# A hybrid decoder layer: two attention rates set to 0.93 and 0.95, and five wide raw-weight buffers in place of four

## The chip, the cores and the metric

The kernel runs on one core of one Trainium2 chip. The metric is the device time of one execution in microseconds (us), the median of three runs. Before the change it is 2094.58 us (2094.41 to 2095.52).

## The reference

One layer over 1024 tokens of width 2048, all in float32:

```python
h = rmsnorm(x, g_pre);  u = h @ w_in          # one projection, its columns cut into parts
log_a = log_sigmoid(g_lr @ w_a2 + b_a) / 16
o_gla = rmsnorm(gla_chunked(gq, gk, gv, log_a), g_head) * silu(g_gate)   # 4 heads, dk 128, dv 256
z = sq @ sk.T * 128**-0.5                                                # 8 heads, dh 128
w = sigmoid(z) * exp(suffix sum of log_sigmoid(-z)), for s < t           # stick-breaking
o_sb = (w @ sv) * silu(s_gate)
x = x + rmsnorm(concat(o_gla, o_sb) @ w_out, g_post)
x = x + sigmoid(x @ w_g + b_g) * (p @ w_p)
```

## The kernel before, in words

Every dense product of float32 is made of three TensorE products. A matrix is split into a rounded part and a rest (`split`: an ACT copy and a DVE subtraction, lines 112 and 113), and rounded x rounded, rest x rounded and rounded x rest are summed in PSUM. Acts are `ah` and `al`; narrow weights are `raw`, split into `hi` and `lo`; wide weights (128x1024, from `wload2`, line 874) are `wr`, split into `wh` and `wl`.

The work has three stretches.

1. **Projections with attention between them.** `dense` runs 38 units of 96 matmuls each, and calls `step()` sixteen times in a unit, once after every six matmuls (the last time behind the evacuation). `step()` adds `rate[1]` to an account and advances the attention's generator once for each whole in it. So `rate[1]` is the number of attention steps for one dense step, and it alone places the attention's instructions among the matmuls. First the four GLA heads come, at rate 1.0, then `sb()`, the stick-breaking attention of eight heads, at 1.0 until the second head's projections are there and at `RATE_SB` from then on. A head can't begin before its three units are done (`while h not in sb_ready`): it spends steps on waiting. A head takes 38 attention steps: 2, and 6 for each of six items. An item is two score blocks one step apart, then, 8 steps after, `turned` (the transposed weights copied and split into `s`, of which there are two pairs of buffers), and 8 further on `values` (the product with v), once or twice (two steps apart).
2. **The end of the attention.** After the last unit, `rate[1]` is `RATE_TAIL`. Twelve small products of the gate's weights (24 matmuls and four steps each) run with what is left of the attention, 48 steps in all. Beside them `x_set` loads eight tiles (`u<-S2x_d`) and splits them (`ah<-u`), then eight of `S1x_d`. What is then left of the attention is written out at once, with no matmul of the products between (line 816: `while urgent or jobs or beside`; called the drain below). Four more small products follow.
3. **Wide products**, one level of a Strassen-like scheme for the gate, `w_out` and `w_g`. `product` takes 24 matmuls; weights are prepared ahead: `wload2` loads, `sub` and `add` (lines 869 and 872) combine blocks, `wsplit` splits. In some loops a round of two products loads three blocks and stores one or two combinations. There are four `wr` buffers. In the last loops `embed` makes six more matmuls from a narrow weight (`pr`, split into `ph` and `pl`).

Nearly all DMAs are issued from SP, in one queue in the order of the program that the scheduler makes (a transpose of attention, `E<-X`, too); ACT, DVE and PE also run in that order. PE's order is that of the steps above.

Of the kernel before, what the change touches and what calls it, by code (L numbers as in the profile page):

```python
# [44 lines left out]

RATE_GLA = 1.0
W0, W1, W2 = 3, 6, 1
RATE_SB = 0.9
W3 = 4
V_MID, V_END, VW = ("X", "X"), ("E", "E"), 3  # L50
L1, L2, PERIOD = 8, 8, 5
# [1 line left out]
KP = KT // 2  # L53
LAG = 10
RATE_BG = 0.5
RATE_TAIL = 1.1
LAST_11 = 4
PACE_QKV, PACE_TAIL = 15, 4

# [2 lines left out]
def layer(ctx, tc, xT, w_in, w_gate, w_lr, w_a2, b_a, g_pre, g_head, w_out, g_post,  # L62
# [24 lines left out]
    def nm(base):  # L87
        serial[0] += 1
        return f"{base}_{serial[0]}"
# [76 lines left out]
    def advance(queue):  # L166
        while queue:
            if next(queue[0], None) is not None:
                return True
            queue.popleft()  # L170
        return False
# [42 lines left out]
    with tc.tile_pool(name="start", bufs=1) as sp:  # L214
# [24 lines left out]
        for q in range(4):  # L239
            w = [wload(w_in[n, q]) for n in range(2)]  # L240
            for kk in range(4):
                k = 4 * q + kk
                sl = slice(kk * P, (kk + 1) * P)
                for hf in HALVES:
                    raw = sp.tile([P, HT], F32, tag="xraw", name=nm("xraw"), bufs=20)
# [30 lines left out]
    with tc.tile_pool(name="att", bufs=1, reuse_waits="tile") as ap:  # L276
# [441 lines left out]
        for u, (h, i) in enumerate(flat):  # L718
# [18 lines left out]
            if i == len(heads[h]) - 1:  # L737
                if h < GLA_HEADS:
                    jobs.append(gla(h, heads[h][0], heads[h][1], heads[h][2:]))
                else:  # L740
                    sb_ready[h - GLA_HEADS] = heads[h]
                    if h == GLA_HEADS:
                        jobs.append(sb())
                    rate[1] = RATE_SB if h > GLA_HEADS else rate[1]

# [10 lines left out]
        def x_set(name, hf):  # L756
            for k in range(8):
                t = at("u")
                dma2(t, part(sx_d[name][k // 2], k))
                yield 1  # L760
                if k % 2 == 0:
                    wides = act_wide(hf, k // 2)
                pair = tuple(part(x, k) for x in wides)
                split(*pair, t)
                g_sets[name].append(pair)
# [38 lines left out]
        while beside:  # L804
            advance(beside)
        rate[1], pace[1] = RATE_TAIL, PACE_TAIL
        beside.append(x_set("S2", 1))
# [17 lines left out]
    def mt(tag, bufs, n=W, dt=F32, name=None):  # L825
        pool = keep if tag == "ar" else mp if tag in ("wr", "wh", "wl", "cw") else late[0]
        return pool.tile([P, n], dt, tag=tag, name=nm(name or tag), bufs=bufs)
# [12 lines left out]
    if True:  # L840
# [31 lines left out]
            V.tensor_tensor(dst, a, b, op=ALU.subtract)  # L872

        def wload2(src):
            raw = mt("wr", 4)
            dma(raw, src)
            return raw

# [142 lines left out]
        for j in range(8):  # L1021
            with ahead():
                b11, t1, t2 = (wload2(w_gate[kh, nh, j]) for kh, nh in ((0, 0), (0, 1), (1, 1)))
                sub(t1, t1, b11)
                sub(t2, t1, t2)
                w2, w1 = wsplit(t2), wsplit(t1)
                add(b11, b11, t2)
                dma2(t2_d[j], t2)
                dma2(t3_d[j], b11)
            p = product(g_sets["S2"], w2)  # L1030
            with soon():
                add(u(j), p, part(u1_s[j // 2], j) if j < 6 else u(j))
            p = product(g_sets["S1"], w1)
            with soon():
                add(v(j), p, u(j))
# [5 lines left out]
        for j in range(8):  # L1041
            with ahead():
                t4, t2 = wload2(w_gate[1, 0, j]), wload2(t2_d[j])
                add(t4, t4, t2)
                w = wsplit(t4)
            p = product(x_act[1][8:], w)
            with soon():
                add(u(j), p, u(j))
        drain()

        for j in range(8):
            with ahead():
                w = wsplit(wload2(t3_d[j]))
            p = product(sets["S3"], w)
            gate(j, 1, p, u(j))
            gate(8 + j, 1, p, v(j))
# [308 lines left out]
```

## Time and profile before

| | us |
|---|---|
| median of three runs | 2094.58 |
| the profiled execution | 2091.95 |
| its span, first to last instruction | 2089.9 |
| PE busy | 2068.4 |
| DVE busy | 1487.0 |
| ACT busy | 875.6 |

Matmuls overlap in the trace, so PE's busy time isn't its work. What tells whether PE loses time is how far apart matmuls start and how many of them fall into a stretch: a stretch of wide products alone holds 222 in 50 us. The projections end and the end of the attention begins at about 1097 us; the wide products begin at 1203 us.

### The profile page before, as it was taken

The numbers are of one execution on the slowest core, as the hardware profiler recorded it, in microseconds if no ns is written. First come the engines' busy times: TensorE is split into PE (matmuls) and PEld (weight loads), VectorE is DVE, ScalarE is ACT, GpSimd is POOL, SyncE is SP. The second block draws the span as 40 slices with busy tenths as digits, with TensorE's granted clock in tenths as the row PEclk, the third lists the DMA queues.
The fourth block names the chain that finished last, engine by engine and source line by source line (L and its number), as shares of the span: only waits on it lengthen the run. The fifth ranks groups of instructions, "written<-read, shape, count | busy, mean of one in ns | idle before, by whom it ended". The sixth has DMA issues, their size and how long they took to land.

```text
span 2089.9 us, 26754 instructions
## 1 busy us (share of the span) xinstructions
PE 2068.4 (99%) x9712; PEld 1708.3 (82%) x9712; DVE 1487.0 (71%) x2243; ACT 875.6 (42%) x1390; POOL 106.5 (5%) x228
## 2 busy tenths in 40 slices
PE   9999999999999999999999999999999999999998
PEld 6788888888888888888888788888888888787887
DVE  8657777676767667666567667788777787876665
ACT  7433333343455455555456413344233434323332
POOL 3100000000011011101001000000000000000000
PEclk9999999999999999999999999999999999999999
DMA  6222222222244344433336687888877586876663
GB/s 217 69 69 74 85 74 85 67 85 67 72 113 105 93 99 121 107 100 97 78 84 152 211 307 282 317 316 289 329 288 261 182 322 216 304 266 213 226 199 113
DMA packets 229812, 352.81 MB, mean 169 GB/s; under 512 B 124464, under 2 KB 129456, under 8 KB 229680
## 3 DMA queue, kind: packets, MB, share of 16 engines
q1 hardware_dynamic: 229104, 349.01, 52.1%
q10 hardware_dynamic: 576, 2.10, 0.3%
q8 instruction: 76, 1.25, 0.3%
q14 instruction: 56, 0.46, 0.1%
HBM read 249.85 MB, written 73.92 MB: 155 GB/s over the span
## 4 chain that ended last, share of the span: by engine, by line
PE 50%; DVE 9%; DMA 8%; issue 2%; ACT 2%; POOL 0%; SPq 0%; DVEq 0%; ACTq 0%; POOLq 0%
PE dn L101 45%; DMA wr<-w_g 3%; PE z L101 2%; PE t L101 2%; DVE wl L113 2%; DMA E<-X 2%; DMA wr<-w_out 1%; PE o L101 1%; DVE wr L872 1%; DVE al L113 1%; DMA ar<-og_d 1%; DVE ar L869 1%; DVE X L599 1%; DVE wr L869 1%; DVE ev L869 0%
## 5 line engine op out<-in xcount | busy, mean ns | idle before, releaser
L101 PE MATMUL dn<-ah,hi 128*128 128x512 f32 x1408 | 563.2, 400 | 1.5 <-ACT hi L112 1.3
L101 PE MATMUL dn<-al,hi 128*128 128x512 f32 x1408 | 551.0, 391 | 0.2 <-DVE al L253 0.2
L101 PE MATMUL dn<-ah,lo 128*128 128x512 f32 x1408 | 550.8, 391 | 0.2 <-DVE lo L113 0.2
L101 PE MATMUL dn<-ah,wl 128*128 128x512 f32 x1216 | 474.1, 390 | 2.2 <-DVE wl L113 2.2
L101 PE MATMUL dn<-al,wh 128*128 128x512 f32 x1216 | 473.7, 390 | 0.0
L101 PE MATMUL dn<-ah,wh 128*128 128x512 f32 x1216 | 473.7, 390 | 0.0
L101 PEld LDWEIGHTS dn<-ah,hi 128*128 128x128 f32 x1408 | 265.8, 189 | 60.7 <-ACT ah L252 3.4
L101 PEld LDWEIGHTS dn<-al,hi 128*128 128x128 f32 x1408 | 264.9, 188 | 58.1 <-DVE al L253 0.9
L101 PEld LDWEIGHTS dn<-ah,lo 128*128 128x128 f32 x1408 | 265.9, 189 | 48.2 <-DVE lo L113 0.5
L112 ACT ACTIVATE wh<-wr 128x1024 fp32r<-128x1024 f32 x152 | 158.9, 1056 | 307.5 <-DVE wr L872 150.1
L101 PEld LDWEIGHTS dn<-ah,wl 128*128 128x128 f32 x1216 | 228.4, 188 | 51.2 <-DVE wl L113 4.0
L101 PEld LDWEIGHTS dn<-ah,wh 128*128 128x128 f32 x1216 | 228.4, 188 | 47.6
L101 PEld LDWEIGHTS dn<-al,wh 128*128 128x128 f32 x1216 | 228.4, 188 | 47.0
L113 DVE TENSOR_TENSOR wl<-wr,wh 128x1024 fp32r<-128x1024 f32 x152 | 185.1, 1219 | 6.5 <-ACT wh L112 6.4
L112 ACT ACTIVATE hi<-raw 128x512 fp32r<-128x512 f32 x192 | 119.8, 626 | 147.3 <-PE dn L101 141.2
L113 DVE TENSOR_TENSOR lo<-raw,hi 128x512 fp32r<-128x512 f32 x192 | 134.7, 703 | 57.7 <-ACT hi L112 57.3
L329 ACT ACTIVATE X<-E 128x256 uint16<-128x256 uint16 (+2 forms) x96 | 81.0, 843 | 126.5 <-DVE E L604 118.9
L599 DVE TENSOR_TENSOR_SCAN X<-X 128x128 f32<-128x128 f32 (+2 forms) x96 | 98.3, 1024 | 30.9 <-POOL X L593 21.0
L872 DVE TENSOR_TENSOR wr<-wr,wr 128x1024 f32<-128x1024 f32 x48 | 58.7, 1224 | 76.4 <-issue 25.0
L614 DVE COPY v<-E 128x512 uint16<-128x512 uint16 (+1 forms) x160 | 63.6, 429 | 55.6 <-DMA E<-X 45.8
L869 DVE TENSOR_TENSOR wr<-wr,wr 128x1024 f32<-128x1024 f32 x48 | 58.8, 1224 | 46.9 <-DMA wr<-w_g 31.8
L113 DVE TENSOR_TENSOR s<-v,s 128x512 fp32r<-128x512 f32 (+1 forms) x82 | 52.3, 638 | 43.2 <-ACT s L112 39.6
(245 smaller groups left out, 2293.0 us busy)
## 6 DMA issues: line engine op xcount, KB each, us to landing
raw<-w_in SPq DMA_DIRECT2D x160, 256.0 KB, 2.7
wr<-w_g SPq DMA_DIRECT2D x64, 512.0 KB, 4.3
wr<-w_out SPq DMA_DIRECT2D x56, 512.0 KB, 4.8
wr<-w_gate SPq DMA_DIRECT2D x40, 512.0 KB, 5.2
g_d<-wr SPq DMA_DIRECT2D x32, 512.0 KB, 2.7
wr<-g_d SPq DMA_DIRECT2D x32, 512.0 KB, 4.9
ar<-h_d SPq DMA_DIRECT2D x28, 512.0 KB, 5.0
ar<-og_d SPq DMA_DIRECT2D x25, 512.0 KB, 4.8
```

The source lines that it names most:

```text
L101: PE.matmul(o, lhsT, rhs, start=start, stop=stop)
L112: A.activation(hi, src, AF.Copy)
L113: (eng or V).tensor_tensor(lo, src, f(hi), op=ALU.subtract)
L329: A.activation(pl.rearrange("p (two n) -> p two n", two=2), src.bitcast(U16)[:, :2 * n].rearrange("p (n two) -> p two n", two=2), AF.Copy)
L599: V.tensor_tensor_scan(rev, rev, rev, initial=kq[:, n:n + 1], op0=ALU.mult, op1=ALU.bypass)
L614: V.tensor_copy(to[:, :, :m, j], w[:, :, 2 * g:2 * g + m])
L869: V.tensor_tensor(dst, a, b, op=ALU.add)
L872: V.tensor_tensor(dst, a, b, op=ALU.subtract)
```

## The change

The attention's rate in its later heads is 0.93 for 0.9, and at its end 0.95 for 1.1. `wr` has five buffers for four; a buffer takes 4 KB of each partition, of which 512 bytes come from the scratch for DMA descriptors, which is set to half. Nothing else changes: the same instructions compute the same values.

```diff
-RATE_SB = 0.9
+RATE_SB = 0.93
...
-RATE_TAIL = 1.1
+RATE_TAIL = 0.95
...
         def wload2(src):
-            raw = mt("wr", 4)
+            raw = mt("wr", 5)
...
-                   dynamic_dma_scratch_size=1024)
+                   dynamic_dma_scratch_size=512)
```

## Rows read from the trace of the kernel before

**Rows 1.** The page: busy time of each engine; and two of its costliest groups of instructions (count, busy us, mean ns of one, idle time before them and who ended it).

```profile
PE 2068.4 (99%) x9712; PEld 1708.3 (82%) x9712; DVE 1487.0 (71%) x2243; ACT 875.6 (42%) x1390; POOL 106.5 (5%) x228
...
L112 ACT ACTIVATE hi<-raw 128x512 fp32r<-128x512 f32 x192 | 119.8, 626 | 147.3 <-PE dn L101 141.2
...
L113 DVE TENSOR_TENSOR s<-v,s 128x512 fp32r<-128x512 f32 (+1 forms) x82 | 52.3, 638 | 43.2 <-ACT s L112 39.6
```

**Rows 2.** The table of stretches: us from the span's start, the stretch's length, then busy us and count of PE, PEld, DVE, ACT, POOL, the granted TensorE clock (1.00 is full), DMA share, GB/s.

```profile
1150.00:1200.00 50.00, 45.95 (x205) 37.54 (x205) 29.96 (x49) 20.57 (x36) 0.00 (x0) 0.93 0.69 211
1250.00:1300.00 50.00, 50.00 (x222) 41.45 (x221) 36.40 (x35) 14.90 (x15) 0.00 (x0) 1.00 0.77 282
1800.00:1850.00 50.00, 47.93 (x209) 38.72 (x208) 45.90 (x51) 16.24 (x22) 0.00 (x0) 1.00 0.82 281
1850.00:1900.00 50.00, 48.50 (x215) 39.85 (x214) 27.95 (x29) 10.50 (x10) 0.00 (x0) 1.00 0.64 222
```

**Rows 3.** Who waited for whom, PE alone, in the attention's heads (580 to 1097 us): us in total, times, longest us.

```profile
PE z L101 <- ACT E L589: 1.4, 3, 0.8
PE z L101 <- DVE u L113: 1.4, 1, 1.4
```

**Rows 4.** The same at the end of the attention (1097 to 1203 us).

```profile
PE t L101 <- ACT s L112: 2.5, 1, 2.5
PE dn L101 <- ACT hi L112: 1.3, 1, 1.3
PE dn L101 <- DVE lo L113: 0.2, 1, 0.2
```

**Rows 5.** PE's timeline from 1156 to 1170 us: start, us, what (in brackets the idle time before it and who ended it).

```profile
1156.74 0.39 PE L101 MATMUL dn<-al,hi 128*128 128x512 f32 x1
1158.42 0.49 PE L101 MATMUL dn<-ah,hi 128*128 128x512 f32 x1 [1.28 <-ACT hi L112]
...
1159.48 0.39 PE L101 MATMUL dn<-al,hi 128*128 128x512 f32 x1
...
1160.17 0.40 PE L101 MATMUL dn<-al,hi 128*128 128x512 f32 x1
1163.11 1.95 PE L101 MATMUL t<-s,u 128*128 128x256 f32 x6 [2.54 <-ACT s L112]
1164.85 0.63 PE L101 MATMUL dn<-ah,hi 128*128 128x512 f32 x1
...
1168.69 0.46 PE L101 MATMUL dn<-ah,hi 128*128 128x512 f32 x1
```

**Rows 6.** The table of stretches again, around that place.

```profile
1156.00:1163.00 7.00, 3.06 (x11) 1.64 (x10) 4.12 (x6) 5.07 (x8) 0.00 (x0) 0.93 0.48 121
1163.00:1169.00 6.00, 5.89 (x17) 4.75 (x18) 4.78 (x10) 3.15 (x7) 0.00 (x0) 0.52 0.96 249
```

**Rows 7.** PE's timeline from 1122 to 1151 us: score blocks (the first of three matmuls of each) and one group of values with the matmul behind it.

```profile
1125.15 0.39 PE L101 MATMUL z<-b,st 128*128 128x512 f32 x1
...
1135.97 0.39 PE L101 MATMUL z<-q,st 128*128 128x512 f32 x1
...
1150.05 0.88 PE L101 MATMUL t<-s,u 128*128 128x256 f32 x6
1150.76 0.40 PE L101 MATMUL dn<-ah,hi 128*128 128x512 f32 x1
```

**Rows 8.** ACT's timeline from 1127 to 1158 us: the first and the last of four score blocks that follow each other (`X<-z`; two more lie between, at roughly even distances), and what came at 1153 us.

```profile
1127.87 0.58 ACT L588 ACTIVATE X<-z 128x512 f32<-128x512 f32 x1
...
1144.04 0.58 ACT L588 ACTIVATE X<-z 128x512 f32<-128x512 f32 x1
...
1153.41 0.63 ACT L112 ACTIVATE ah<-u 128x512 fp32r<-128x512 f32 x1 [3.12 <-DMA u<-S2x_d]
1153.94 0.58 ACT L588 ACTIVATE X<-z 128x512 f32<-128x512 f32 x1
...
1156.79 1.06 ACT L329 ACTIVATE X<-E 128x1024 uint16<-128x1024 uint16 x1 [1.78 <-DVE E L604]
1157.75 0.61 ACT L112 ACTIVATE hi<-raw 128x512 fp32r<-128x512 f32 x1
```

**Rows 9.** SP's timeline at that time.

```profile
1148.26 1.24 SPq L332 DMA_TRANSPOSE E<-X  x1
1149.56 0.57 SPq L759 DMA_DIRECT2D u<-S2x_d  x1
```

**Rows 10.** Who waited for whom, PE alone, in the wide products (1203 to 2090 us).

```profile
PE dn L101 <- DVE wl L113: 2.2, 2, 1.5
PE o L101 <- DVE pl L113: 1.4, 1, 1.4
PE z L101 <- DVE pl L113: 1.1, 2, 0.7
```

**Rows 11.** Who waited for whom, SP's queue, in the loop from 1825 to 1915 us that loads three blocks a round.

```profile
SPq L876 <- DVE wl L113: 21.1, 16, 4.1
SPq L1259 <- DVE wr L872: 18.9, 6, 5.3
```

**Rows 12.** DVE's timeline from 1872 to 1898 us: ahead of the longer of the two waits for `wl`.

```profile
1894.49 1.22 DVE L872 TENSOR_TENSOR wr<-wr,wr 128x1024 f32<-128x1024 f32 x1 [4.71 <-DMA wr<-w_g]
1895.63 1.22 DVE L113 TENSOR_TENSOR wl<-wr,wh 128x1024 fp32r<-128x1024 f32 x1
```

## The prediction

> **What bounds the kernel now.** I read the page first: PE is busy for 99% of the span, DVE for 71%, ACT for 42% [rows 1]. So TensorE's work is the floor and neither edit changes that work; only places where PE stands still can be won, and the question is how many there are. The table of stretches says where. A stretch of wide products alone holds 222 matmuls in 50 us [rows 2], so one takes 50 / 222 = 0.225 us and a step of six 1.35 us. The stretch at 1150 us holds 205 at a granted clock of 0.93, those at 1800 and 1850 us hold 209 and 215 [rows 2]; the others are full. Then the waits of PE in three stretches: 2.8 us in the attention's heads [rows 3], 4.0 us at its end [rows 4], 4.7 us in the wide products [rows 10]. With what the clock takes (below) that is some 14 us, 0.7% of the time, and the edits can reach no more than that.
>
> The end of the attention is the largest piece, and its timeline shows a chain. From 1156.74 to 1159.48 us PE does three matmuls, 2.74 - 3 x 0.225 = 2.06 us lost, waiting for the split of a narrow weight [rows 5]. From 1160.17 to 1163.11 us it waits for `s`, the split attention weights: 2.94 - 0.23 = 2.71 us lost [rows 5]. Behind that the granted clock is 0.52 [rows 6], which is the lower of the two levels, 1.2 GHz in place of 2.4: six matmuls of values take 1.74 us [rows 5] where the same six took 0.71 us [rows 7], and nine dense ones 3.84 us [rows 5] for 9 x 0.225 = 2.03 us. The clock costs 1.03 + 1.81 = 2.84 us. Together 2.06 + 2.71 + 2.84 = 7.6 us.
>
> Why was `s` late? ACT's timeline: score blocks follow each other in (1144.04 - 1127.87) / 3 = 5.39 us [rows 8], though PE had them ready long before: the block made at 1125.15 us is the second of these four, the one of 1135.97 us the last, taken up at 1144.04 us [rows 7, 8], 8 us late. So sigmoid, scan, product, rounding copy and transpose form a chain that takes 5.39 us a block, 10.8 us an item of two. Then ACT stands 3.12 us at `ah<-u`, whose load SP issued only at 1149.56 us, behind a transpose that itself waited for that chain [rows 8, 9]; a weight's `hi` stands behind all of it, at 1157.75 us [rows 8], and PE needed it at 1156.97 us.
>
> **The change part by part.**
>
> *Rate 0.95 at the end.* An item is six attention steps. At 1.1 it gets 6 / 1.1 = 5.45 dense steps, 7.4 us, and its own matmuls: two blocks of three, 1.35 us, and two groups of values, 1.42 us [rows 2, 7]. That is 10.1 us for a chain that needs 10.8: attention falls behind by 0.6 us an item. At 0.95 it gets 6.32 steps, 8.5 + 2.8 = 11.3 us, so it catches up. Counting the loop's steps by hand (38 units x 16 = 608, then 48 to 656), the last head begins at step 609 under both rates; the next to last item's first values move from step 647 to 653, its score blocks only from 633 to 636. Three steps more, 4 us, lie between them, which is more than the 2.71 us missing. The wait for `s` goes, and with it the low clock: -2.71 - 2.84 = -5.55 us. The wait for `hi` I leave where it is: the eighth load of `x_set` is written at step 640 under both rates with its split directly behind it, and ACT will still stand at it. Bounds for that piece: -2.06 to 0 us.
>
> What is late next: 48 x 0.95 is 45.6 attention steps where 1.1 gave 52.8, and the head needs 51. Five steps are left to the drain, and both groups of values of the last item stand behind the last dense step with nothing between. `s` has two pairs of buffers: the last group's split can begin only when the group at step 655 has been multiplied, and then PE has one step and one group ahead of it, 1.35 + 0.71 = 2.06 us [rows 2, 7]. The split takes an ACT copy of about 0.63 us and a DVE subtraction of 0.64 us, 1.27 us [rows 1], if nothing is in front. Two other splits in front, 0.63 us each, make it 0.5 us late, three 1.1 us; a load like the one of 3.12 us [rows 8] makes it 2.3 us late. Between 0 and 2.3 us I take 0.8 us, nearest to the rows of single splits.
>
> *Rate 0.93 in the heads.* An item gets 6 / 0.93 = 6.45 steps, 8.7 + 2.8 = 11.5 us, where 0.9 gave 11.8; the chain's 10.8 us still fits. A head has 38 attention steps and a new one arrives every 48 dense steps; 38 / 0.9 = 42.2 and 38 / 0.93 = 40.9. By the count, heads 4 to 7 begin at steps 465, 513, 561 and 609 under both rates: they wait for their projections, and the rate only makes the wait longer. Only heads 1 to 3 run closer. Cost 0; bounds: -2.8 us if both waits of [rows 3] go, +2.8 us if as much is added.
>
> *Five buffers for wide raw weights.* In a loop with three loads a round four buffers hold one block of the next round. SP's queue stands for a buffer to come free behind the `wl` split, 21.1 us in 16 waits of this 90 us loop, and for a store behind a subtraction, 18.9 us [rows 11]; whatever is queued behind the load on SP waits with it. DVE then stands for the load, 4.71 us ahead of the subtraction at 1894.49 us, `wl` follows at 1895.63 us [rows 12], and PE waits for it. A fifth buffer lets the load go out one release earlier, and releases in this loop are several us apart, more than the 1.5 us that PE waited. Both waits for `wl`, 2.2 us, go. The waits for `pl`, 1.4 + 1.1 us [rows 10], come in loops where DVE is busy for 45.9 of 50 us [rows 2] and the narrow weight's split stands in its queue; I leave them. Bounds: -4.7 us (all of rows 10) to +2.8 us (below, the last rival, at two waits). The load of buffers and the two adds and stores are the same as before; the scratch feeds no DMA here, as the page's list of DMAs names SP and ACT alone: 0.
>
> One rule speaks against this part. PE's waits in 880 us of wide products are five, at different places, two of them for `wl` [rows 10]. The Trainium skill, "Perfetto Trace Analysis", under "Optimization Strategy", takes a gap that repeats through a stretch on the engine that should be saturated as the sign that buffers are too few. Read strictly, the fifth buffer then brings nothing: that is the second rival. The repeating gap here is DVE's and SP's, not PE's.
>
> **The sum.** -5.55 + 0.8 (end of the attention) + 0 (heads) - 2.2 (buffers) = -6.95 us. The profiled execution took 2091.95 us, 2089.9 of span and 2.05 around it; by the sum it would take 2085.0. It lies 2.63 us under the median of three, so the forecast for the median is 2094.58 - 6.95 = 2087.6 us. With the bounds of the `hi` wait and of the drain (2.3 for 0.8) its own range is 2084 to 2090.4.
>
> **The rivals.**
>
> *The wait moves to the drain.* The last `s` is late by 2.3 us in place of the earlier 2.71, and the clock falls as before, 2.84 us. The end of the attention then gives back 5.1 of 5.55 us: 2094.58 - 0.4 - 2.2 = 2092.0 us. For it: two buffer pairs, and only one dense step of cover. Against it: the chain has caught up by then.
>
> *The fifth buffer brings nothing.* PE waits where DVE's order puts the work late, and buffers don't change DVE's work. 2094.58 - 4.75 = 2089.8 us.
>
> *Everything goes*, the `hi` and `pl` waits too, and the drain costs nothing: 2094.58 - 7.6 - 4.7 = 2082.3 us.
>
> *SP's single queue turns against the change.* An earlier weight load stands ahead of the narrow loads of `embed` in SP's order and waits there for its buffer; `pr` comes later, and PE waits for `pl`, 1.4 us each as once now [rows 10]. There are 32 such weights. Four waits eat the 4.75 us of the attention's end, from the seventh on the kernel is slower by over 0.2%; at eight it takes 2094.58 - 4.75 + 11.2 = 2101.0 us. For it: SP already stands for `wr` slots most of the time [rows 11], so what is behind is late by as much. Against it: a fifth buffer also makes each such stand shorter.
>
> That the rates don't do what they say is half true already: the one of the heads moves only heads 1 to 3.
>
> **How the numbers follow.** Forecast 0.38, the drain 0.22, the buffer without effect 0.15, everything 0.10, SP's queue 0.15. A measurement of this kernel can tell about 0.2%, 4.2 us, from no change: 2090.4 and 2098.8 are the borders. Faster: 0.34 of the forecast, all of "everything", half of the buffer case, 0.34 + 0.10 + 0.07 = 0.51. Slower: most of SP's queue, 0.13. Within: the rest, 0.36. For eight in ten the range runs from 2082.3, the case in which everything goes, to 2098, which leaves out most of SP's queue and the half of the lowest case.
>
> **What would show it.** Right: no PE wait for `s` near 1160 us and no stretch at the low clock there; PE idle for `wl` near 1497 and 1895 us gone, and SP's loads of `wr` issued two ahead of a round; score blocks of the last head taken up less than 5 us after PE made them. Wrong: a wait for `s` or a low clock just behind the last dense step of the attention, new waits for `z` in heads 1 to 3, or more waits for `pl` than three. What would make the forecast wrong altogether is a different order by the scheduler in the wide products, which a fifth buffer can bring about anywhere in 880 us.

## The result, and the profile after

The changed kernel takes 2102.26 us (median of 8 runs, 2098.72 to 2105.85), the kernel before 2094.49 us beside it (8 runs, 2090.36 to 2096.31): ratio 1.0034, 95% interval 1.0023 to 1.0046. It is slower by some 7 to 8 us, where 7 us less were forecast; the time lies outside the range. The profiled execution is a long one, 2105.85 us with a span of 2103.8, while that of before was a short one, so the two traces differ by 13.9 us, more than the medians do.

The page first: PE has the same 9712 matmuls and 2.8 us more of busy time than in [rows 1]. No work was added; PE stands still more.

```profile
PE 2071.2 (98%) x9712; PEld 1711.5 (81%) x9712; DVE 1490.3 (71%) x2243; ACT 879.5 (42%) x1390; POOL 113.8 (5%) x228
```

PE's waits by stretch (us in total, times, longest). In the heads, against [rows 3]:

```profile
PE z L101 <- DVE u L113: 3.8, 2, 2.4
```

At the end of the attention, against [rows 4]:

```profile
PE t L101 <- ACT s L112: 5.2, 2, 4.3
PE dn L101 <- ACT hi L112: 1.2, 2, 0.6
PE dn L101 <- DVE lo L113: 1.2, 2, 0.9
PE t L101 <- DVE s L113: 0.3, 1, 0.3
```

In the wide products, against [rows 10]:

```profile
PE o L101 <- DVE pl L113: 3.5, 1, 3.5
PE t L101 <- DVE pl L113: 2.8, 2, 2.1
PE z L101 <- DVE pl L113: 2.5, 2, 1.5
PE t L101 <- ACT ph L112: 2.2, 2, 2.0
PE dn L101 <- DVE wl L113: 0.5, 2, 0.3
```

Heads 3.8 for 2.8 us, end 7.9 for 4.0, `wl` 0.5 for 2.2, `pl` and `ph` 11.0 for 2.5: 11.7 us more. What is left of the 13.9 us fits the clock behind the longest waits. The table of stretches shows it at four places (length, busy us and counts, granted clock, DMA share, GB/s): nearly full PE stretches at 0.69, 0.76, 0.72 and 0.54, the lower of the two levels for part of each.

```profile
644.00:648.00 4.00, 4.00 (x14) 3.29 (x14) 3.48 (x10) 1.55 (x6) 1.08 (x5) 0.69 0.07 16
...
1182.00:1190.00 8.00, 7.41 (x28) 6.17 (x29) 3.28 (x5) 3.04 (x7) 0.00 (x0) 0.76 0.75 236
...
1834.00:1840.00 6.00, 5.92 (x19) 4.72 (x20) 6.00 (x8) 1.53 (x2) 0.00 (x0) 0.72 0.86 276
...
1996.00:2002.00 6.00, 5.35 (x13) 4.21 (x14) 3.36 (x6) 0.42 (x1) 0.00 (x0) 0.54 0.35 109
```

The first of them lies in the heads, behind the longer of the two waits there. PE's timeline of the changed kernel has this row:

```profile
642.86 0.33 PE L101 MATMUL z<-u,st 128*128 128x128 f32 x1 [2.42 <-DVE u L113]
```

The kernel before waited 1.37 us at that place and kept its clock. This is the same stretch of it:

```profile
644.00:648.00 4.00, 3.94 (x19) 3.16 (x20) 3.69 (x9) 2.00 (x8) 1.38 (x5) 1.00 0.16 55
```

**The end of the attention.** The earlier wait for `s`, at 1160 us in [rows 5], is gone. In its place PE's timeline shows one just behind the last dense step, in the drain:

```profile
1173.62 0.80 PE L101 MATMUL t<-s,u 128*128 128x256 f32 x6
...
1175.46 0.40 PE L101 MATMUL dn<-al,hi 128*128 128x512 f32 x1
1176.70 0.50 PE L101 MATMUL t<-s,u 128*128 128x256 f32 x2 [0.84 <-ACT s L112]
1177.51 0.74 PE L101 MATMUL t<-s,u 128*128 128x256 f32 x4 [0.30 <-DVE s L113]
1182.59 1.95 PE L101 MATMUL t<-s,u 128*128 128x256 f32 x6 [4.34 <-ACT s L112]
```

There is one dense step between (1174.26 to 1175.46 us); then two groups of values follow each other. ACT's timeline says why their `s` was late. Ahead of the first, ACT stood 1.22 us at the split of a narrow weight, and ahead of the last 2.49 us at a split of the second `x_set`; neither load had landed. The last `s` then waited another 1.62 us for `v`, which DVE copies.

```profile
1175.50 0.63 ACT L112 ACTIVATE hi<-raw 128x512 fp32r<-128x512 f32 x1 [1.22 <-DMA raw<-w_gate]
1176.04 0.61 ACT L112 ACTIVATE s<-v 128x512 fp32r<-128x512 f32 x1
1179.14 0.63 ACT L112 ACTIVATE ah<-u 128x512 fp32r<-128x512 f32 x1 [2.49 <-DMA u<-S1x_d]
...
1181.91 0.63 ACT L112 ACTIVATE s<-v 128x512 fp32r<-128x512 f32 x1 [1.62 <-DVE v L614]
```

DVE's timeline has the other half of that `x_set` split, which waited with ACT, and behind it the two copies into `v`, with the rest (`lo`) of a narrow weight between them:

```profile
1179.80 0.69 DVE L113 TENSOR_TENSOR al<-u,ah 128x512 fp32r<-128x512 f32 x1 [2.35 <-ACT ah L112]
1180.41 0.45 DVE L614 COPY v<-E 128x512 uint16<-128x512 uint16 x1
...
1181.35 0.45 DVE L614 COPY v<-E 128x512 uint16<-128x512 uint16 x1
```

So one load held both engines, and 2.0 us of DVE's queue (1179.80 to 1181.80 us) came on top of ACT's stand.

**The embedding's narrow weights.** At 1985 us SP's timeline shows two wide loads ahead of a narrow one:

```profile
1985.02 0.33 SPq L876 DMA_DIRECT2D wr<-u_d  x1
1986.15 0.33 SPq L876 DMA_DIRECT2D wr<-w_g  x1
1986.59 0.38 SPq L1179 DMA_DIRECT2D pr<-w_p  x1
```

ACT's timeline has the split that the narrow load releases; it begins 1993.61 - 1986.59 = 7.0 us after the load was issued:

```profile
1993.61 0.42 ACT L112 ACTIVATE ph<-pr 128x256 fp32r<-128x256 f32 x1 [3.87 <-DMA pr<-w_p]
```

And PE's timeline the two waits that follow from it:

```profile
1994.07 0.50 PE L101 MATMUL t<-ph,ph 128*128 128x512 f32 x1 [2.03 <-ACT ph L112]
1996.65 0.80 PE L101 MATMUL t<-ph,pl 128*128 128x512 f32 x1 [2.07 <-DVE pl L113]
```

### The profile page after: what moved, and what is told of

The parts are those of the page before. It is cut to its first block, busy times and chain, and to the rows that moved or that the text cites. A ratio compares the mean times of both kernels' runs of the same rounds, so it can differ in the third digit from the quotient of the medians.

```text
span 2103.8 us, 26752 instructions
## 1 busy us (share of the span) xinstructions
PE 2071.2 (98%) x9712; PEld 1711.5 (81%) x9712; DVE 1490.3 (71%) x2243; ACT 879.5 (42%) x1390; POOL 113.8 (5%) x228
## 4 chain that ended last, share of the span: by engine, by line
PE 79%; DMA 9%; DVE 7%; issue 2%; ACT 2%; SPq 0%; DVEq 0%; POOL 0%; ACTq 0%
PE dn L101 69%; PE z L101 5%; PE t L101 2%; PE o L101 2%; DMA wr<-w_g 2%; DVE wl L113 1%; DMA E<-X 1%; DMA ar<-h_d 1%; DMA cw<-og_d 1%; DMA wr<-w_out 1%; DMA h_d<-st 1%; DVE ar L872 1%; DVE wr L869 1%; DMA raw<-w_gate 1%; DVE wr L872 0%
## 5 line engine op out<-in xcount | busy, mean ns | idle before, releaser
L112 ACT ACTIVATE ah<-ar 128x1024 fp32r<-128x1024 f32 x46 | 48.8, 1062 | 91.4 <-DVE ar L872 39.2
```

Of the source, the lines that this page charges most:

```text
L112: A.activation(hi, src, AF.Copy)
```

## The experiments

Each was timed in rounds beside the kernel before, on the same chip; ratios have 95% intervals. The four groups of runs were on four chips, so between groups the ratios compare, not the times. The theory to begin with: both parts cost, at two places that have nothing to do with each other. The rivals: the buffer alone, or the rates alone.

**The rates alone** (the two lines of the diff that set them).

> The two rates alone (0.93 and 0.95), four wide buffers and the full scratch as before. Theory 1 (both parts cost: the rates some 4 us at the end of the attention, where the last values now stand in the drain; the fifth buffer some 4 to 8 us in the loops with narrow embedding weights): +3 to +5 us against the kernel before, the wide loops as before with about 5 us of waits of PE. Theory 2 (the fifth buffer is the whole loss, the rates do what was forecast in the median and the profiled execution was an odd one): -5 to 0 us. Theory 3 (the rates are the whole loss): +7 to +9 us.

2095.48 us, ratio 1.0014 (1.0004 to 1.0025). PE waits 5.4 us for `s` at the end of the attention and 6.6 us in the wide products.

**The fifth buffer alone** (`mt("wr", 5)`, half the scratch).

> The fifth wide buffer alone (with half the scratch), rates 0.9 and 1.1 as before. Theory 1: +4 to +8 us, waits of PE for wl under 1 us in total, and for pl and ph in the embedding loops 8 us or more where before had 2.5 us; the end of the attention as before, with about 7.6 us lost. Theory 2: +7 to +9 us. Theory 3: -3 to 0 us.

2095.41 us, ratio 1.0016 (1.0007 to 1.0024). Its PE waits behind 1760 us, 8.4 us in place of 2.5:

```profile
PE z L101 <- DVE pl L113: 2.9, 2, 2.7
PE t L101 <- DVE pl L113: 2.1, 1, 2.1
PE o L101 <- DVE pl L113: 2.0, 1, 2.0
PE t L101 <- ACT ph L112: 1.4, 1, 1.4
```

So each part costs about 3 us by its ratio, and together 6.3 of the 7.1 us that the ratio of the change makes. Theories 2 and 3 fall. The order of instructions agrees: behind 1760 us SP's and DVE's order is that of before in the kernel with the rates alone, and another in the one with the buffer.

**Each rate alone.**

> Only the rate at the end of the attention, 0.95 for 1.1. Theory 1: the whole of the rates' cost sits in the drain, so +3 to +4 us, with a wait of PE for s of over 3 us just behind the last dense step and a low clock there. Rival: the rate of the heads carries it (heads 1 to 3 wait for the second split of k), then 0 us or a gain here.

> Only the rate in the later heads, 0.93 for 0.9. Theory 1: heads 4 to 7 begin where they did, so within 1 us of the kernel before, and waits of PE between 580 and 1097 us of 2.5 to 4 us. Rival (the heads carry the cost of the rates): +2 us or more.

0.95 at the end: 2094.46 us, ratio 1.0014 (1.0003 to 1.0024), with the wait for `s` in the drain, 5.9 us in two. 0.93 in the heads: 2094.9 us, ratio 1.0014 (1.0003 to 1.0024), PE's waits in the heads 3.4 us, near the changed kernel's 3.8, with the clock at 0.69 from 644 to 648 us again. That both alone cost what they cost together didn't fit; the last runs come back to it. The trace with 0.93 alone shows one thing more: at rate 1.1 PE has no wait for `s` at the end of the attention, neither near 1160 us nor later. So 0.93 in the heads takes the earlier wait away too, which was not forecast.

**The scratch alone.**

```diff
-                   dynamic_dma_scratch_size=1024)
+                   dynamic_dma_scratch_size=512)
```

> The kernel before with half the scratch for DMA descriptors and nothing else: the same instructions in the same order on every engine. If the scratch is idle, as GpSimd issues no DMA, the time is that of the kernel before (within 0.1%), and the run also shows how far apart two like kernels are measured. Rival: the addresses matter, and the 3 us of the fifth buffer belong to the scratch: +2 to +4 us.

2094.24 us, ratio 0.9999 (0.9988 to 1.0009). It costs nothing that can be told. The same instructions showed 4.2 us of PE waits for `wl` and `wh` in the wide products where the trace of before has 2.2: one trace of such waits is one draw.

**The narrow load first,** beside the fifth buffer. In `embed`:

```diff
-                with tc.high_priority(offset=400):
+                with tc.high_priority(offset=1000):
                     dma2(wr, w_p[n])
```

> Five wide buffers and rates as before, and the narrow embedding weight is loaded with a higher priority (1000 for 400), so that SP issues its load ahead of the wide loads that the fifth buffer had let past it. If the order of the loads is what the fifth buffer cost, PE's waits for pl and ph behind 1760 us fall from 8.4 us to 3 us or less, and the time lies 3 to 6 us under the fifth buffer alone (2095.4): 2089 to 2092. Rival: DVE's queue holds the narrow split whatever SP does, as it is busy for 46 of 50 us there; then the waits stay at 6 to 9 us and the time within 1 us of 2095.4.

2089.12 us, ratio 0.9971 (0.9960 to 0.9982), 4.5 parts in a thousand under the buffer alone. PE's waits behind 1760 us:

```profile
PE o L101 <- DVE pl L113: 2.2, 1, 2.2
PE z L101 <- DVE pl L113: 1.2, 1, 1.2
PE t L101 <- DVE pl L113: 0.4, 1, 0.4
```

SP's timeline at the place that stood at 1985 us above: now `pr` goes ahead of both wide loads.

```profile
1974.18 0.38 SPq L1179 DMA_DIRECT2D pr<-w_p  x1
1976.57 0.33 SPq L876 DMA_DIRECT2D wr<-u_d  x1
1977.70 0.33 SPq L876 DMA_DIRECT2D wr<-w_g  x1
```

That settles what the buffer cost: its wide loads had taken the place of a small load in one queue. That the gain of 0.29% is the buffer's own was argued, not shown, because no run has the narrow load first with four buffers. For it: the waits for `pl` and `ph` are 3.8 us here, where the trace of before has 2.5 and the scratch run's 3.4, so putting the load first only restored them, while the waits for `wl` and `wh` are gone. Against it: in the eight traces with five buffers these are 0 to 3.9 us behind 1203 us, in the nine with four 0.8 to 5.8, so they overlap.

**The drain.** First its last loop alone, at rate 0.95:

```diff
-            advance(beside)
-            advance(urgent) or advance(jobs)
+            advance(urgent) or advance(jobs) or advance(beside)
```

> Rate 0.95 at the end of the attention alone, and in the drain the attention's last steps are written ahead of the remaining loads and splits of x_set (before, one of each in turn). If ACT's stand at such a load in front of the last s split is the cost of 0.95, the wait for s behind the last dense step falls from 5.8 us to 1 to 2 us and the clock stays up there: 3 to 4 us less than 0.95 alone, 2090 to 2091.5. Rival: two pairs of s buffers and one dense step of cover are the cause; then the wait stays over 4 us and the time at 2094 to 2095.

2097.29 us, ratio 1.0011 (1.0002 to 1.0021); the wait for `s` stays, 5.6 us. But the edit hadn't moved what it meant to: ACT's timeline still has 3.66 us at an `ah<-u` ahead of the `s` split, as with the rate alone, whose rows are these:

```profile
1174.49 0.63 ACT L112 ACTIVATE ah<-u 128x512 fp32r<-128x512 f32 x1 [4.03 <-DMA u<-S1x_d]
...
1175.54 0.61 ACT L112 ACTIVATE s<-v 128x512 fp32r<-128x512 f32 x1
```

The order of ACT, DVE and SP is that of the rate alone until 1180 us, so the run decides nothing. **The whole second `x_set` behind the attention** does move it:

```diff
-        beside.append(x_set("S1", 0))
...
-        while urgent or jobs or beside:
-            advance(beside)
-            advance(urgent) or advance(jobs)
+        while urgent or jobs:
+            advance(urgent) or advance(jobs)
+        for _ in x_set("S1", 0):
+            pass
```

> Rate 0.95 at the end alone, and the loads and splits of the second x_set (S1) are written behind all of the attention, so that no split that waits for such a load stands in front of the last s on ACT. The drain edit alone had left such a split in front (ACT stood 3.7 us at it), and the wait with it. If ACT's stand is the cost of 0.95, the wait for s behind the last dense step falls from 5.6 us to under 2 us, the clock stays at 1.00 there, and the time is 3 to 5 us under 0.95 alone: 2090 to 2092, or -4 to 0 us against the kernel before. Rival: the two pairs of s buffers with one dense step of cover are enough to cause it; then over 4 us of wait stay and the time is +1 to +4 us against the kernel before.

2092.07 us, ratio 0.9988 (0.9977 to 1.0000), 2.6 parts in a thousand under the rate alone. The `ah` splits are gone from ACT there, but 4.3 us of waits for `s` stay, 3.4 of them in one: ACT now stands at the next things in its order that wait for a load, the narrow weights, twice ahead of that `s`.

```profile
1171.00 0.63 ACT L112 ACTIVATE hi<-raw 128x512 fp32r<-128x512 f32 x1 [1.98 <-DMA raw<-w_gate]
1173.48 0.63 ACT L112 ACTIVATE hi<-raw 128x512 fp32r<-128x512 f32 x1 [1.84 <-DMA raw<-w_gate]
1174.02 0.61 ACT L112 ACTIVATE s<-v 128x512 fp32r<-128x512 f32 x1
```

The time is what the theory said. The trace is not: over 4 us of waits stay, as the rival had it, and the granted clock is 0.51 from 1176 to 1182 us.

**Rate 1.06 at the end,** with nothing left to the drain.

> Rate 1.06 at the end of the attention, all else as before: by the count of steps nothing is left to the drain, and an item gets 6 / 1.06 x 1.35 + 2.8 = 10.4 us, where 1.1 gave 10.1 and the chain needs 10.8. If the drain is what 0.95 costs, no wait for s behind the last dense step of over 2 us, and the time is -3 to 0 us against the kernel before. Rival (any change of the rate disturbs the loads' order in the wide loops and costs 3 us): +2 to +4 us.

2090.81 us, ratio 0.9979 (0.9967 to 0.9991); PE's waits from 1097 to 1190 us are 2.1 us, 1.2 of them for `s`.

**Both mends together.**

> Five wide buffers with half the scratch, the narrow embedding weight loaded at the higher priority, rate 1.06 at the end, 0.9 in the heads. If the two gains (-0.29% and -0.21%) lie in different stretches and add up: 2094.4 - 10.5 = 2083 to 2086 us, ratio 0.994 to 0.996. Rival: what the one saves the other's shift of the order gives back: 2087 to 2090.

> As the version with five buffers, the narrow weight first and rate 1.06, and the second x_set (S1) written behind the attention too. If ACT's stand at its loads still costs at 1.06 (some 1 to 2 us of waits for s and hi there), 1 to 3 us less than without: 2081 to 2085 us. Rival: at 1.06 the attention has time enough, or the late splits delay the first wide product: 0 to +3 us against it.

Buffer, narrow load first and 1.06: 2089.06 us, ratio 0.9976 (0.9963 to 0.9988); the gains don't add up. With the second `x_set` late as well: 2086.39 us, ratio 0.9961 (0.9947 to 0.9975). The intervals of these two overlap.

**The changed kernel, mended** in one place and in both.

> The changed kernel (0.93, 0.95, five buffers, half the scratch) with one thing more, the higher priority of the narrow embedding weight's load. If the loads' order is what the fifth buffer cost, and the rates cost what they cost alone (+3 us), 5 to 7 us under the changed kernel: 2094 to 2097 us, ratio 0.999 to 1.001, with waits for pl and ph behind 1770 us of 4 us or less (11 before the edit). Rival: the waits were an odd execution's; then 2100 us or more.

2096.14 us, ratio 0.9994 (0.9981 to 1.0008): the narrow load first gives the changed kernel 4 parts in a thousand back, and its waits for `pl` and `ph` behind 1760 us are 3.5 us for 11.0.

> The changed kernel (0.93, 0.95, five buffers, half the scratch) with the narrow weight's load first and the second x_set behind the attention. If the loads' order and ACT's stand were the two costs, 3 to 5 us under the version with the narrow weight first alone: 2091 to 2093 us, ratio 0.997 to 0.999. Rival (the drain costs by itself, whatever stands in front of s): 2095 to 2097, ratio 0.999 to 1.001, with a wait for s of over 4 us.

2085.43 us, ratio 0.9960 (0.9945 to 0.9974), better than expected and below both kernels. Beside the run before it this is one edit, and the intervals lie apart (0.9981 to 1.0008, and 0.9945 to 0.9974). With rate 0.95 and five steps left to the drain, PE's waits for `s` are down to these, and the clock stays at 1.00 from 1165 to 1187 us:

```profile
PE t L101 <- ACT s L112: 0.8, 1, 0.8
PE t L101 <- DVE s L113: 0.5, 2, 0.3
```

In place of the two stands ahead of the first late `s` in the run with 0.95 and four buffers, ACT's timeline has one of that size:

```profile
1170.14 0.63 ACT L112 ACTIVATE hi<-raw 128x512 fp32r<-128x512 f32 x1 [1.92 <-DMA raw<-w_gate]
1170.68 0.62 ACT L112 ACTIVATE s<-v 128x512 fp32r<-128x512 f32 x1
```

The edit moves the loads of the second `x_set` in SP's queue as well as its splits on ACT and DVE; how much each of the two gives was not separated.

**What was left open.**

> The fastest version so far (five buffers, narrow weight first, 1.06 at the end, second x_set late) with 0.93 in the heads. If 0.93 costs by itself, as alone (+1.4 parts in a thousand), ratio 0.997 to 0.9985 where that version had 0.9961, with waits for z behind DVE's u of 3.5 us or more in the heads (1.3 there). Rival (it cost only through the end of the attention): ratio 0.995 to 0.9965.

2086.8 us, ratio 0.9964 (0.9952 to 0.9975), beside 0.9961 with 0.9 in the heads. That is in the rival's range, though PE waits 3.7 us for `z` behind DVE's `u` in the heads, as the theory had it. The two intervals overlap so far that a cost of 1.4 parts in a thousand isn't excluded.

> The kernel before with the second x_set behind the attention, rate 1.1, four buffers. The last load of the first x_set, at which ACT stood 3.1 us, stays where it is. If that stand and the chain of attention that can't follow 1.1 make the waits near 1156 us, they stay, and the time is within 2 us of the kernel before. Rival (it is the second x_set that delays the last items at any rate): -3 to -6 us, as 0.95 gained by it.

2095.35 us, ratio 1.0004 (0.9991 to 1.0016). At 1.1 moving the second `x_set` gives nothing; the waits near 1160 us are those of [rows 4] to a tenth:

```profile
PE t L101 <- ACT s L112: 2.5, 1, 2.5
PE dn L101 <- ACT hi L112: 1.3, 1, 1.3
```

## Why the prediction was wrong

*Where PE loses time* was right: 99% busy, and all that moved was a dozen waits and the clock behind them.

*The rate at the end, first half* came out, but half of the reason given for it did not. The wait for `s` at 1160 us went in every kernel with 0.95; with 1.1 and 0.9 in the heads it stayed, 2.5 us in each of five traces, and with 1.1 and 0.93 it went as well. So each of the two rates takes it away alone. And that attention falls behind at 1.1 and catches up at 0.95 is not what the rows show: before, the second blocks of three items in a row were taken up 6.6, 8.4 and 8.1 us after PE made them, in the changed kernel 7.3, 8.6 and 8.2 us (the last of these made at 1140.23, taken up at 1148.42 us). The wait for `hi` stayed in the changed kernel, as forecast, though behind a load of the second `x_set`, at which ACT stood 4.21 us until 1158.32 us, not of the first.

*What is late next* is the first step that failed: "Between 0 and 2.3 us I take 0.8 us". The mechanism was named, the size was not: 5.5 us of waits for `s`, with the low clock behind. I priced one thing in front of the last split, and the bound was built from one row of a stand, 3.12 us. The stand itself was shorter, 2.49 us. What the price left out stood around it: the split before had been held 1.22 us by another load, and behind the stand DVE did 2.0 us of work in its order before the copy into `v` was there that `s` is split from. The sum of the bound (copy, subtraction and stand less 2.06 us of cover) has no term for either. With the second set's loads and splits moved behind the attention and the narrow load first, the waits were 1.3 us, inside the bounds.

*Five buffers* is the second. The 2.2 us for `wl` came off in the profiled execution (0.5 left), but not reliably: in three of the later traces with five buffers PE waits 2.0, 3.4 and 3.9 us for it. And "the waits for `pl` I leave them" was wrong: with `ph` they went from 2.5 to 11.0 us. I had the mechanism as the last rival, SP's single queue, at 0.15, with eight waits of 1.4 us, and it came as seven waits of up to 3.5 us with two stretches of low clock. The argument that made it small, that a fifth buffer shortens each stand of SP, looks at the wide loads alone. A wide load that goes out earlier also takes DMA time ahead of the small load that PE needs next (7.0 us until its split began, above, where 3.3 us is the median to landing).

*The rivals* were held to exclude each other. They sit 800 us apart and both came true, so their prices add: about 3 us each by the single runs, and the two gains they swallowed. A case "both" had no chance at all in the sum. The forecast's own range was added up wrongly too: with the bounds named for it (2.06 us less for `hi`, 0.8 less or 1.5 more for the drain) it is 2084.8 to 2089.1 us, not 2084 to 2090.4. The measured time lies outside either.

*The scratch* at 0 was right: 0.9999. *The heads* at 0 weren't shown to be: alone 0.93 measured 1.0014, beside the mended parts 0.9964 for 0.9961. The sign of being wrong that was named, new waits for `z`, came: in the changed kernel 2.42 us for 1.37 at 643 us, and 1.35 us at 715 us where there had been none. The clock fell behind the longer of them, for which the prediction had no term; it is 0.50 to 0.69 from 644 to 648 us in all six traces with 0.93, and 1.00 in the eleven with 0.9. *The rule on repeating gaps* of the Trainium skill ("Perfetto Trace Analysis", "Optimization Strategy") didn't decide. It says that such a gap can mean too few buffers, not that without one there are enough, and the prediction read it the second way. PE's gaps weren't a repeating pattern, yet five buffers with the narrow load first measured 0.9971.

Half open: why 0.93 in the heads, alone, measured 1.0014. Its trace has 0.6 us more of waits in the heads than before, and from 640 to 648 us the clock (0.88, then 0.69 over 4 us each) takes 1.7 us by an estimate from these two figures, together of the size measured. On the other side the wait for `s` at the end and the low clock behind it are gone from that trace, so how the parts add up was not shown.

Why 4.3 us of waits for `s` stayed with 0.95 and four buffers and 1.3 us in the mended changed kernel, which has the same rate and the same edit there, shows in the two traces. With 0.9 in the heads PE has no dense step between the first two of the last three groups of values; with 0.93 it has one (1169.64 to 1171.34 us), and ACT has one narrow weight's split less, with its stand, ahead of the first late `s`. The rates alone, with four buffers, have that dense step too, so it comes with the rate of the heads. The prediction had treated the two rates as separate parts.

## What to carry to other kernels

When one queue feeds an engine, more buffers for its large loads is a change of order: look which small load, needed sooner, will now stand behind them, and raise it first. When a wait is removed by shifting work later, price the new place by all that stands in front of it in every in-order engine that it passes: a stand at a load on the one, and what the other must still do behind the same load. Two rivals at different places can both come true; give "both" a chance and add their prices.

## What the runs showed that I had not expected

A 128 KB load, 3.3 us from issue to landing at the median of the changed kernel, released its split only 7.0 us after issue where two 512 KB loads had been issued 1.6 and 0.4 us before it; the longest landing of such a load in that trace is 6.9 us. And a wait can cost more than its length: behind the 4.34 us for `s` and the 2.03 and 2.07 us for the narrow weight the granted clock was 0.76 and 0.54 over stretches of 8 and 6 us, while in the mended kernel, whose waits for `s` were 0.8 us and less, it stayed at 1.00 there. Executions of the same program differ by 10 us and more (the kernel before: 2087.76 to 2101.30 in 35 runs). Such waits come and go: the trace of before has 11.5 us of PE waits, that of the same instructions with half the scratch 15.0 us in an execution 4.2 us longer. The trace on which the forecast rested was one of the shorter ones.
